# The MLP's second product by Strassen's scheme, its MLP stage issued in a planned order

## The chip, the cores and the metric

The kernel runs on one core of a Trainium2 chip. The metric is device time in microseconds from the start to the end of one execution. TensorE (PE) multiplies, with its weight loads (PEld) alongside; VectorE (DVE), ScalarE (ACT) and GpSimd (POOL) do elementwise work; SyncE (SP) issues most of the transfers.

## The reference: what is computed

One decoder layer on x of 512 tokens x 1024 channels, all in float32. A normalised x is projected; half of the columns go through block-sparse attention, half through a causal convolution; both are joined, projected and added to x. What the change touches is the rest:

```python
hn = rms_norm(h, g_mlp_norm[l])
ff = jnp.square(jax.nn.relu(hn @ w_mlp_in[l]))     # 512x1024 @ 1024x4096
h = h + ff @ w_mlp_out[l]                          # 512x4096 @ 4096x1024
return rms_norm(h, g_final)
```

## The kernel before, in words

Every float32 product is made of three passes. An operand `v` is split into a high part (a cast to fp32r, on ACT) and a low part (`v` minus the high part, on DVE), and `mm3` adds high x high, high x low and low x high in PSUM (lines 263 to 265). So each weight tile costs one cast (L236) and one subtraction (L237) of 128x1024 elements, and each product three matmuls.

The MLP goes through the 4096 hidden channels in 4 chunks of 1024 (`NCH`, `CHUNK` = 8 blocks of 128). In a chunk, 8 hidden blocks are made, each a `block` of 8 x 3 matmuls of 512 columns into one PSUM bank (tiles `ff`), and `relu_square` (L999 to L1003) makes of each the relu on ACT, the square on DVE, the high part on ACT and the low part on DVE. The second product of the chunk follows (`zmm`, tiles `z`): for each half of the 1024 output columns, 4 token tiles x 8 blocks x 3 matmuls of 512 columns, which makes 192 a chunk. DVE adds the four banks of a half to the residual `xr` (L1078). Weights arrive through 4 raw buffers and 3 pairs of split buffers, always in the order of `srcs`.

The order of the MLP's instructions is the order in which the code is written. The stages before it are issued by a planner (`Plan`), which picks the next step from costs, due times and biases by kind (`BIAS`); the MLP is not planned in the kernel before. The last half of the last chunk does one token tile after another, with the last tile in two pieces of 256 columns, so that the final norm (L1087, L1022, L1023, L945, L1032) and the stores of a tile run beside the matmuls of the next.

Of the kernel before, what the change touches and what calls it, by code (L numbers as in the profile page):

```python
# [10 lines left out]
F32 = mybir.dt.float32  # L11
# [6 lines left out]
P = 128  # L18
# [14 lines left out]
SCRATCH = 4096  # L33
CT = 4
# [28 lines left out]
class Plan:  # L63
# [32 lines left out]
    def run(self):  # L96
# [8 lines left out]
        while ready:  # L105
            best, first = [], {}
            for s in ready:
                t = 0.0
                ok = True
                for b in s["uses"]:  # L110
                    if b["tag"] is None:
                        f = self.free[b["kind"]]
                        if len(f) <= (s["keep"] if self.hot else 0):
                            ok = False
                            break
                        t = max(t, min(f.values()))
# [46 lines left out]
def hybrid_layer(ctx: ExitStack, tc: tile.TileContext, x, pack, w_in, w_out, g_mlp, w1, w2, g_fin, out):  # L163
# [34 lines left out]
    for c in range(DFF // P // CHUNK):  # L198
        srcs += [colblock(w1, c * CHUNK + b) for b in range(CHUNK)]
        for hf in range(2):  # L200
            srcs += [rowpair(w2, c * CHUNK + k, hf * 512) for k in range(0, CHUNK, 2)]
# [724 lines left out]

    pm.tile([P, 1456], F32, name="shift")
# [211 lines left out]
```

## Time and profile before

| | us |
|---|---|
| runs | 578.13, 579.93, 1454.63 (median 579.93) |
| the profiled execution's own time | 578.81 |
| its span, first to last instruction | 577.1 |
| PE busy | 562.6 (97%) |
| DVE, ACT, POOL busy | 327.2, 264.9, 143.7 |
| a chunk of the MLP, 307 to 394 us: PE, DVE, ACT, POOL busy | 87.00, 36.12, 25.81, 0.00 |
| from the end of the last matmul to the end of the span | 7.1 |

The profiled execution took 578.81 us, 1.1 less than the median; the run of 1454.63 us stands alone. The granted TensorE clock was 0.996 on average. A busy PE is read with care, since matmuls overlap: the step from one start to the next is what one costs. The rows themselves are below, in numbered groups.

### The profile page before, as it was taken

The page shows a single profiled execution, that of the slowest core. Times are in us where ns is not written, and L with a number is a line of the kernel's source. Part 1 is how long each engine was busy: PE and PEld are TensorE (multiplying, and loading weights), DVE is VectorE, ACT ScalarE, POOL GpSimd, SP SyncE. Part 2 cuts the span into 40 slices and gives each one's busy share as a digit, 9 for nine tenths or more (in the row PEclk, how much of TensorE's full clock was granted, in tenths as well). Part 3 has the DMA queues.
Part 4 walks back from the last instruction along what each step waited for, and adds up shares of the span by engine and source line. Part 5 has one row for each costly group of instructions (what it writes and reads, how often), then busy time and mean ns, then how long its engine had stood idle before and what let it go on. Part 6 is the DMA issues. An engine that isn't in the chain of part 4 may idle for free.

```text
span 577.1 us, 7305 instructions
## 1 busy us (share of the span) xinstructions
PE 562.6 (97%) x2784; PEld 472.4 (82%) x2784; DVE 327.2 (57%) x489; ACT 264.9 (46%) x445; POOL 143.7 (25%) x166
## 2 busy tenths in 40 slices
PE   8999999899899999999999999999999999999995
PEld 7988888787688889988888888888888888888884
DVE  4479889899996764544424444324454324454343
ACT  5776596979875442533212343212343212343223
POOL 2289979599645310000000000000000000000002
PEclk9999999999999999999999999999999999999998
DMA  8443323221131720323332323333223323233103
GB/s 274 137 136 94 101 73 110 68 80 37 37 147 39 218 75 1 123 98 109 108 104 79 104 79 110 110 90 92 91 92 109 110 79 104 82 101 110 37 0 148
DMA packets 58836, 56.20 MB, mean 97 GB/s; under 512 B 1840, under 2 KB 42928, under 8 KB 58800
## 3 DMA queue, kind: packets, MB, share of 16 engines
q1 hardware_dynamic: 58512, 54.68, 30.6%
q10 hardware_dynamic: 288, 1.05, 0.5%
q8 instruction: 22, 0.36, 0.2%
q14 instruction: 14, 0.11, 0.1%
HBM read 53.62 MB, written 2.10 MB: 97 GB/s over the span
## 4 chain that ended last, share of the span: by engine, by line
PE 92%; DVE 2%; ACT 2%; DMA 1%; issue 1%; POOL 0%; SPq 0%; POOLq 0%; ACTq 0%
PE ff L264 10%; PE ff L265 10%; PE ff L263 10%; PE z L264 10%; PE z L263 10%; PE z L265 10%; PE u L263 3%; PE u L264 3%; PE u L265 3%; PE y L263 3%; PE y L265 3%; PE y L264 3%; PE q L265 1%; PE q L263 1%; PE v L263 1%; PE q L264 1%
## 5 line engine op out<-in xcount | busy, mean ns | idle before, releaser
L237 DVE TENSOR_TENSOR wl<-raw,wh 128x1024 fp32r<-128x1024 f32 (+1 forms) x69 | 81.4, 1183 | 94.2 <-ACT wh L236 94.0
L236 ACT CAST wh<-raw 128x1024 fp32r<-128x1024 f32 (+1 forms) x73 | 70.9, 981 | 115.2 <-PE z L265 84.0
L263 PE MATMUL ff<-hTh,wh 128*128 128x512 f32 (+1 forms) x280 | 103.9, 371 | 0.0
L264 PE MATMUL ff<-hTl,wh 128*128 128x512 f32 (+1 forms) x280 | 103.8, 371 | 0.0
L265 PE MATMUL ff<-hTh,wl 128*128 128x512 f32 (+1 forms) x280 | 103.8, 371 | 0.0
L264 PE MATMUL z<-wl,ffh 128*128 128x512 f32 (+1 forms) x264 | 101.0, 383 | 0.0
L263 PE MATMUL z<-wh,ffh 128*128 128x512 f32 (+1 forms) x264 | 101.0, 383 | 0.0
L265 PE MATMUL z<-wh,ffl 128*128 128x512 f32 (+1 forms) x264 | 101.0, 383 | 0.0
L550 POOL TENSOR_TENSOR acc<-acc,ct 128x512 f32<-128x512 f32 x60 | 89.2, 1487 | 11.8 <-ACT ct L547 8.5
L937 POOL TENSOR_SCALAR ms0f<-ms_f 128x1 f32<-128x1 f32 x4 | 0.8, 190 | 328.7 <-ACT f L329 328.7
L263 PEld LDWEIGHTS ff<-hTh,wh 128*128 128x128 f32 x280 | 52.8, 188 | 9.1
L264 PEld LDWEIGHTS ff<-hTl,wh 128*128 128x128 f32 x280 | 52.8, 188 | 9.0
L265 PEld LDWEIGHTS ff<-hTh,wl 128*128 128x128 f32 x280 | 52.8, 188 | 9.0
L1001 DVE TENSOR_TENSOR sq<-rl 128x512 f32<-128x512 f32 x32 | 22.2, 693 | 64.2 <-ACT rl L999 64.2
L263 PEld LDWEIGHTS z<-wh,ffh 128*128 128x128 f32 x264 | 49.6, 188 | 9.8
L264 PEld LDWEIGHTS z<-wl,ffh 128*128 128x128 f32 x264 | 49.6, 188 | 9.7
L265 PEld LDWEIGHTS z<-wh,ffl 128*128 128x128 f32 x264 | 49.6, 188 | 9.6
L999 ACT ACTIVATE rl<-ff 128x512 f32<-128x512 f32 x32 | 19.2, 599 | 82.6 <-PE ff L265 82.6
L566 DVE SCALAR_TENSOR_TENSOR cs<-hin,pk,cs 128x512 f32<-128x512 f32 x58 | 43.5, 750 | 0.9
L547 ACT ACTIVATE ct<-hin,pk 128x512 f32<-128x512 f32 x60 | 40.5, 718 | 2.5 <-POOL acc L550 1.8
L1003 DVE TENSOR_TENSOR ffl<-sq,ffh 128x512 fp32r<-128x512 f32 x32 | 22.2, 694 | 21.9 <-ACT ffh L1002 21.9
L453 ACT CAST wh<-raw 128x1024 fp32r<-128x1024 f32 x21 | 22.0, 1050 | 21.7 <-PE u L264 9.9
(172 smaller groups left out, 926.8 us busy)
## 6 DMA issues: line engine op xcount, KB each, us to landing
raw<-w SPq DMA_DIRECT2D x64, 512.0 KB, 3.7
raw<-w_in SPq DMA_DIRECT2D x18, 512.0 KB, 3.6
raw<-w_out SPq DMA_DIRECT2D x8, 512.0 KB, 3.6
xr<-x SPq DMA_DIRECT2D x4, 512.0 KB, 5.1
out<-ot SPq DMA_DIRECT2D x8, 256.0 KB, 2.0
x<-x SPq DMA_DIRECT2D x4, 256.0 KB, 4.6
raw<-w_in SPq DMA_DIRECT2D x4, 256.0 KB, 6.4
x<-x SPq DMA_DIRECT2D x2, 512.0 KB, 6.6
```

Source lines behind the costliest of these rows:

```text
L236: nc.scalar.copy(hi[:, c], raws[n][:, c])
L237: low.tensor_tensor(lo[:, c], raws[n][:, c], f32(hi[:, c]), op=OP.subtract)
L263: nc.tensor.matmul(ps, sh, mh, start=first, stop=False)
L264: nc.tensor.matmul(ps, sh, ml, start=False, stop=False)
L265: nc.tensor.matmul(ps, sl, mh, start=False, stop=last)
L453: nc.scalar.copy(hi, raws[n])
L547: p = plan.step(f"prod{i}", "act", 0.72, lambda src=src, j=j, ct=ct: nc.scalar.activation(get(ct), src, AF.Copy, scale=wtap(i, j)), needs= ...
L550: s = plan.step(f"tapp{i}", "pool", 1.38, lambda ct=ct: nc.gpsimd.tensor_tensor(get(acc), get(acc), get(ct), op=OP.add), needs=[p, s], use ...
L566: s = plan.step(f"tapd{i}", "dve", 0.78, lambda src=src, j=j, last=last: nc.vector.scalar_tensor_tensor(get(acc) if last else get(cs), src ...
L999: nc.scalar.activation(rl, ps, AF.Relu)
L1001: nc.vector.tensor_mul(sq, rl, rl)
L1003: nc.vector.tensor_sub(ff["l"][:, b], sq, f32(ff["h"][:, b]))
```

## The change

The second product of a chunk is a product of a 512x1024 matrix F by a 1024x1024 matrix W. F is cut into 2x2 blocks of (256 tokens x 512 channels), W into 2x2 blocks of (512 channels x 512 columns), and Strassen's seven products take the place of eight: each is a sum or difference of blocks of F times a sum or difference of blocks of W, 2 token tiles x 4 channel blocks x 3 matmuls of 512 columns. A chunk has 168 of these for 192 before. In turn

- blocks of W are added and subtracted before they are split (`mt1`, `mt3`, `mt4`, `mt6`, `mt7`, two 128x1024 halves each), and 14 tiles of the second product's weights are split, for 8 before (`mb`);
- F is kept as float32, and its 7 operands (5 of them sums or differences, `ms`) are split as 128x1024 tiles (`ma`), where before each of 8 hidden blocks was split at 128x512;
- each product lands in two banks and is added to, or subtracted from, one to two blocks of the residual: 24 additions of 128x512 a chunk for 8 (`mev`);
- the square is one DVE instruction that reads PSUM and the relu.

Every step of the MLP is handed to the planner, with `ON` naming kinds that go to one engine only. As the planner assigns them, 7 sums of a chunk are on POOL (mt3 and mt6 and mt1, two each, and ms7); in the last chunk two low parts as well. The rest is on DVE.

```diff
+ON = {
+    "mal": ("dve",), "ms1": ("dve",), "ms5": ("dve",), "ms6": ("dve",), "ms7": ("pool",), "mt1": ("pool",),
+    "mt3": ("pool",), "mt6": ("pool",), "mt7": ("dve",),
+}
...
+    "low15": -172, "max": -20, "max4": -63, "max5": -116, "max6": -30, "mbh": -377, "mbl": -249.6, "mev": -240.1,
+    "mfo": -646, "ms1": 261, "norm": 453, "os": 122, "os4": -49, "pl": 80, "pl3": -53, "prod": -356,
...
-    pm.tile([P, 1456], F32, name="shift")
+    pm.tile([P, SHIFT], F32, name="shift")
...
-    def relu_square(c, b, ps):
-        rl = pm.tile([P, S], F32, tag="rl", name=f"rl{c}_{b}", bufs=2)
-        nc.scalar.activation(rl, ps, AF.Relu)
-        sq = pm.tile([P, S], F32, tag="sq", name=f"sq{c}_{b}", bufs=2)
-        nc.vector.tensor_mul(sq, rl, rl)
-        nc.scalar.copy(ff["h"][:, b], sq)
-        nc.vector.tensor_sub(ff["l"][:, b], sq, f32(ff["h"][:, b]))
...
+    def combine(kind, out, a, b, op, needs, uses):
+        def fn():
+            e = nc.gpsimd if s["eng_used"] == "pool" else nc.vector
+            e.tensor_tensor(out(), a(), b(), op=op)
+
+        s = plan.step(kind, either(kind), 0, fn, needs=needs, uses=uses, shared=True)
+        return s
+
+    def weights(kind, b, ready, a):
+
+        wb = plan.buffer("w", w_tiles)
+        h = plan.step(f"{kind}h", "act", 1.04, lambda: nc.scalar.copy(get(wb)[0], get(b)), needs=[ready, last.get("high")], uses=[b, wb])
+        last["high"] = h
+        l = low_parts(f"{kind}l", lambda: get(wb)[1], lambda: get(b), lambda: get(wb)[0], [h], [b, wb])
...
+    def operand(kind, ob, i, x, needs, uses):
+
+        hi, lo = (lambda: quarter(ob, i)), (lambda: quarter(ob, i + 1))
+        h = plan.step(f"{kind}h", "act", 1.04, lambda: nc.scalar.copy(hi(), x()), needs=needs, uses=uses + [ob])
+        l = low_parts(f"{kind}l", lo, x, hi, [h], uses + [ob])
...
+    def add_to(t, cols, b, needs, op=OP.add):
+        n = cols.stop - cols.start
+        return plan.step("mev", "dve", dve_cost(n), lambda: nc.vector.tensor_tensor(
+            xt[t][:, cols], xt[t][:, cols], get(b)[:, 0:n], op=op), needs=needs, uses=[b])
...
+        return plan.step("msq", "dve", 0.75, lambda: nc.vector.scalar_tensor_tensor(
+            get(F)[:, b % 4], get(ps), 0.0, get(rl), op0=OP.max, op1=OP.mult), needs=[s], uses=[ps, rl, F])
...
+        s3 = sums("mt3", t3, r12, r22, OP.subtract, [row("12"), row("22")])
+        B[3] = split(t3, s3)
+        s6 = sums("mt6", r12, r12, r11, OP.add, [s3, row("11")])
+        B[6] = split(r12, s6)
+        t4 = [new_tt(f"t4{j}_{c}") for j in js]
+        s4 = sums("mt4", t4, r21, r11, OP.subtract, [row("21"), row("11")])
+        B[4] = split(t4, s4)
+        B[2] = split(r11, row("11"))
+        s1 = sums("mt1", r11, r11, r22, OP.add, [low_of(2), row("22"), s6, s4])
+        B[1] = split(r11, s1)
+        B[5] = split(r22, row("22"))
+        s7 = sums("mt7", r21, r21, r22, OP.add, [s4, row("22")])
+        B[7] = split(r21, s7)
...
-        for hf in range(2):
-            cols = slice(hf * 512, (hf + 1) * 512)
...
-            for kp in range(0, tail, 2):
-                w = unit()
-                for k in (kp, kp + 1):
-                    for ps, (t, pc) in zip(banks, pieces):
-                        zmm(ps, k, t, w, k == 0, k == CHUNK - 1, pc)
...
+        O = {3: operand("ma", ops[0], 0, A(0, 0), k1, [F[0]])}
...
+        mixed(6, 1, 0, 2, A(1, 0), A(0, 0), OP.subtract, k1, [F[0]])
+        O[4] = operand("ma", ops[1], 0, A(1, 1), k2, [F[1]])
+        mixed(2, 0, 1, 2, A(1, 0), A(1, 1), OP.add, k2, F)
+        mixed(1, 1, 2, 0, A(0, 0), A(1, 1), OP.add, k2, F)
+        mixed(5, 0, 2, 2, A(0, 0), A(0, 1), OP.add, k2, F)
+        mixed(7, 1, 3, 0, A(0, 1), A(1, 1), OP.subtract, k2, [F[1]])
...
+                            mm3(get(banks[t])[:, 0:cols.stop - cols.start], ah[:, k, ts], al[:, k, ts], bh[:, kk, cols],
+                                bl[:, kk, cols], k == 0, k == 3)
...
+        spread(3, (0, 1, add), (1, 1, add))
+        spread(6, (1, 1, add))
+        spread(4, (0, 0, add), (1, 0, add))
+        spread(2, (1, 0, add), (1, 1, sub))
+        spread(1, (1, 1, add), (0, 0, add))
+        if not final:
+            spread(5, (0, 0, sub), (0, 1, add))
+            spread(7, (0, 0, add))
+            return
...
+    for c in range(NCH):
+        chunk(c)
+    for s in plan.run():
+        s["fn"]()
```

The products run in the order 3, 6, 4, 2, 1, 5, 7. Each has two halves (j = 0, 1), which need one split weight tile each; a half is 12 matmuls. The instructions of all engines ahead of the MLP stand as before, and so do the matmuls of the first chunk's hidden blocks.

Place 1 is DVE in the third chunk, from the square of the last hidden block up to the last operand that the first products need. Before, behind the last square and its low part, only the low parts of weights and the four residual additions follow:

```order
L1001 TENSOR_TENSOR sq_7_4016<-rl_7_4014 128x512
L1003 TENSOR_TENSOR ffl_3723<-sq_7_4016,ffh_3722 128x512
L237 TENSOR_TENSOR wl_4025<-raw_3877,wh_4024 128x1024
L237 TENSOR_TENSOR wl_4055<-raw_3914,wh_4054 128x1024
L237 TENSOR_TENSOR wl_4085<-raw_3951,wh_4084 128x1024
L237 TENSOR_TENSOR wl_4115<-raw_3988,wh_4114 128x1024
L1078 TENSOR_TENSOR xr<-xr,z_4020 128x512
```

Now twelve instructions of 128x1024 follow the last square, which itself writes F_2_4033. The first two are the sums for products 1 and 2; op... are low parts of operands of F (opxl of products 4 and 2, opffh of 1 and 5); wl<-r_2_3886 is the second half's weight of product 6, t_2_... those of product 4, r_3884 and r_3925 those of product 2:

```order
L1066 TENSOR_TENSOR temp_4002<-F_2_3882,F_2_4033 128x1024
L1066 TENSOR_TENSOR temp_4143<-F_2_3882,F_2_4033 128x1024
L1058 TENSOR_TENSOR opxl<-F_2_4033,opxl 128x1024
L1058 TENSOR_TENSOR opffh<-temp_4002,opffh 128x1024
L1058 TENSOR_TENSOR opxl<-temp_4143,opxl 128x1024
L1058 TENSOR_TENSOR wl<-r_2_3886,wh 128x1024
L1066 TENSOR_TENSOR temp_4143<-F_2_3882,F_2_4033 128x1024
L1058 TENSOR_TENSOR wl<-t_2_3998,wh 128x1024
L1058 TENSOR_TENSOR wl<-t_2_4068,wh 128x1024
L1058 TENSOR_TENSOR opffh<-temp_4143,opffh 128x1024
L1058 TENSOR_TENSOR wl<-r_3884,wh 128x1024
L1058 TENSOR_TENSOR wl<-r_3925,wh 128x1024
```

What moved: the low part that product 6 needs halfway stands sixth behind the last square, and those of product 2 eleventh and twelfth.

Place 2 is the weight of product 1. It is a sum that POOL writes over r_3884 and r_3925 once product 2's low parts have been made of them, and behind it POOL has the sum for product 7. POOL's whole list for the third chunk (before, POOL had nothing in the MLP until the final norm):

```order
L1066 TENSOR_TENSOR t_2_3888<-r_2_3845,r_2_3879 128x1024
L1066 TENSOR_TENSOR r_2_3845<-r_2_3845,r_3884 128x1024
L1066 TENSOR_TENSOR t_2_3955<-r_2_3886,r_2_3921 128x1024
L1066 TENSOR_TENSOR r_2_3886<-r_2_3886,r_3925 128x1024
L1066 TENSOR_TENSOR r_3884<-r_3884,r_2_3879 128x1024
L1066 TENSOR_TENSOR r_3925<-r_3925,r_2_3921 128x1024
L1066 TENSOR_TENSOR temp_4002<-F_2_4033 128x1024
```

On DVE, the two low parts of product 1's weight stand among residual additions (m_4153 is product 6, m_4191 product 4); four additions of product 3 (m_4108, m_4112) stand ahead of these rows:

```order
L1092 TENSOR_TENSOR xr<-xr,m_4153 128x512
L1092 TENSOR_TENSOR xr<-xr,m_4157 128x512
L1092 TENSOR_TENSOR xr<-xr,m_4191 128x512
L1058 TENSOR_TENSOR wl<-r_3884,wh 128x1024
L1092 TENSOR_TENSOR xr<-xr,m_4195 128x512
L1092 TENSOR_TENSOR xr<-xr,m_4191 128x512
L1058 TENSOR_TENSOR wl<-r_3925,wh 128x1024
L1058 TENSOR_TENSOR wl<-r_2_3879,wh 128x1024
```

What moved: a weight that was a load, a cast and a subtraction now waits for DVE, then POOL, then ACT, then DVE again.

Place 3 is the end on DVE. Before, the last token tile alone is left when the last matmuls run:

```order
L1087 TENSOR_TENSOR xr<-xr,z_4729 128x256
L945 SCALAR_TENSOR_TENSOR ot_4716<-xr,fr_4865,gfinbc 128x512
L1087 TENSOR_TENSOR xr<-xr,z_4730 128x256
L1022 SCALAR_TENSOR_TENSOR fs_768_4903,ms_f_768_4904<-xr 128x256
L1023 TENSOR_TENSOR fn_768_4902<-ms_f_768_4904,fn_512_4884 128x1
L945 SCALAR_TENSOR_TENSOR ot_4724<-xr,fr_4907,gfinbc 128x512
```

Now (m_4950 and m_4982 are the first tile and the first half of the second tile of product 7, mlast the second half; ahead of these rows stand the four additions of product 5, one of product 1 and one scaled output):

```order
L1092 TENSOR_TENSOR xr<-xr,m_4950 128x512
L1145 TENSOR_TENSOR ot_4989<-xr,gfinbc 128x512
L1092 TENSOR_TENSOR xr<-xr,m_4982 128x256
L1145 TENSOR_TENSOR ot_4989<-xr,gfinbc 128x512
L1179 SCALAR_TENSOR_TENSOR ot_4989<-xr,fr_2538,gfinbc 128x512
L1092 TENSOR_TENSOR xr<-xr,mlast 128x256
L1145 TENSOR_TENSOR ot_5036<-xr,gfinbc 128x512
L1166 SCALAR_TENSOR_TENSOR fs_256_5040,ms_f_256_5039<-xr 128x256
L1168 TENSOR_TENSOR fn_256_2542<-ms_f_256_5039,fn_0_2541 128x1
L1145 TENSOR_TENSOR ot_5036<-xr,gfinbc 128x512
L1179 SCALAR_TENSOR_TENSOR ot_5036<-xr,fr_2540,gfinbc 128x512
L1179 SCALAR_TENSOR_TENSOR ot_5036<-xr,fr_2543,gfinbc 128x512
```

What moved: more of the final norm stands behind the last matmul on DVE, and the stores of two tiles instead of one.

## Rows read from the trace of the kernel before

**Rows 1.** The page's busy us, share of the span and instructions of each engine.

```profile
PE 562.6 (97%) x2784; PEld 472.4 (82%) x2784; DVE 327.2 (57%) x489; ACT 264.9 (46%) x445; POOL 143.7 (25%) x166
```

**Rows 2.** The page's chain of waits that ended last, share of the span by engine.

```profile
PE 92%; DVE 2%; ACT 2%; DMA 1%; issue 1%; POOL 0%; SPq 0%; POOLq 0%; ACTq 0%
```

**Rows 3.** Stretches: length, busy us (instructions) of PE, PEld, DVE, ACT, POOL; clock, DMA share, GB/s.

```profile
307.00:394.00 87.00, 87.00 (x386) 72.06 (x384) 36.12 (x41) 25.81 (x32) 0.00 (x0) 1.00 0.32 97
...
139.00:148.00 9.00, 7.58 (x51) 5.85 (x49) 8.65 (x23) 7.92 (x20) 8.20 (x11) 1.00 0.35 118
```

**Rows 4.** Instructions on PE in order of time: start us, us, what; second and third chunk's first matmul.

```profile
308.32 0.39 PE L263 MATMUL ff<-hTh,wh 128*128 128x512 f32 x1
...
395.36 0.39 PE L263 MATMUL ff<-hTh,wh 128*128 128x512 f32 x1
```

**Rows 5.** Groups by line and shape: count, busy us, mean ns, idle before.

```profile
L237 DVE TENSOR_TENSOR wl<-raw,wh 128x1024 fp32r<-128x1024 f32 x65 | 79.6, 1225 | 94.1 <-ACT wh L236 94.0
L1001 DVE TENSOR_TENSOR sq<-rl 128x512 f32<-128x512 f32 x32 | 22.2, 693 | 64.2 <-ACT rl L999 64.2
L1078 DVE TENSOR_TENSOR xr<-xr,z 128x512 f32<-128x512 f32 x28 | 19.1, 687 | 7.6 <-PE z L265 7.6
L728 DVE SCALAR_TENSOR_TENSOR vhl<-v,r,vhl 128x512 fp32r<-128x512 f32 x4 | 3.0, 748 | 0.8 <-ACT vhl L725 0.8
L236 ACT CAST wh<-raw 128x1024 fp32r<-128x1024 f32 x65 | 68.3, 1050 | 115.2 <-PE z L265 84.0 <-DVE xr L1078 17.5 <-issue 10.2
L457 POOL TENSOR_TENSOR wl<-raw,wh 128x1024 fp32r<-128x1024 f32 x1 | 2.4, 2406 | 0.0
```

**Rows 6.** In order of time, behind one hidden block: PE's next matmul, ACT, DVE.

```profile
400.80 0.39 PE L263 MATMUL ff<-hTh,wh 128*128 128x512 f32 x1
...
401.00 0.60 ACT L999 ACTIVATE rl<-ff 128x512 f32<-128x512 f32 x1 [4.38 <-PE ff L265]
...
401.63 0.69 DVE L1001 TENSOR_TENSOR sq<-rl 128x512 f32<-128x512 f32 x1 [3.76 <-ACT rl L999]
```

**Rows 7.** In order of time, DVE instructions one behind the other.

```profile
41.52 1.55 DVE L566 SCALAR_TENSOR_TENSOR cs<-hin,pk,cs 128x512 f32<-128x512 f32 x2
...
85.65 1.22 DVE L457 TENSOR_TENSOR wl<-raw,wh 128x1024 fp32r<-128x1024 f32 x1
86.78 0.75 DVE L566 SCALAR_TENSOR_TENSOR cs<-hin,pk,cs 128x512 f32<-128x512 f32 x1
87.44 0.69 DVE L685 TENSOR_TENSOR ql<-tpq,qs 128x512 fp32r<-128x512 f32 x1
```

**Rows 8.** Single lines in the convolution stage: duration ns min/median/max, first and last start.

```profile
L457 DVE TENSOR_TENSOR wl<-raw,wh x20: 1214/1352/2328, 26.7 to 142.1; 128x1024 fp32r<-128x1024 f32 x20
...
L550 POOL TENSOR_TENSOR acc<-acc,ct x60: 1272/1295/2244, 32.0 to 142.5; 128x512 f32<-128x512 f32 x60
```

**Rows 9.** In order of time, DVE reading PSUM beside POOL's one 128x1024 instruction.

```profile
177.26 2.94 DVE L865 TENSOR_SCALAR y<-cp,mv,r_ln 128x512 f32<-128x512 f32 x4
...
178.55 2.41 POOL L457 TENSOR_TENSOR wl<-raw,wh 128x1024 fp32r<-128x1024 f32 x1
```

**Rows 10.** In order of time, the end: last matmuls, DVE's last instructions, the last store's issue.

```profile
569.59 0.28 PE L264 MATMUL z<-wl,ffh 128*128 128x256 f32 x1
569.71 0.28 PE L265 MATMUL z<-wh,ffl 128*128 128x256 f32 x1
...
570.36 0.42 DVE L1087 TENSOR_TENSOR xr<-xr,z 128x256 f32<-128x256 f32 x1
...
572.31 0.75 DVE L945 SCALAR_TENSOR_TENSOR ot<-xr,fr,gfinbc 128x512 f32<-128x512 f32 x1 [0.67 <-POOL fr L1027]
...
573.49 0.37 SPq L1034 DMA_DIRECT2D out<-ot  x1
```

**Rows 11.** The page's transfers: KB each, median us from issue to landing.

```profile
raw<-w SPq DMA_DIRECT2D x64, 512.0 KB, 3.7
out<-ot SPq DMA_DIRECT2D x8, 256.0 KB, 2.0
```

More of the change, by code (lines that the diff above doesn't have):

```diff
@@ L109, in run @@
                 ok = True
[L110 to L116, printed above, removed]
+                new = [b["kind"] for b in s["uses"] if b["tag"] is None]
+                for kind in new:
+                    f = sorted(self.free[kind].values())
+                    n = new.count(kind)
+                    if len(f) < n + (s["keep"] if self.hot else 0):
+                        ok = False
+                        break
+                    t = max(t, f[n - 1])
                 if not ok:
@@ L1029, in final_store, with either @@
[L1029 to L1038 removed]
+    def either(kind):
+        costs = {"dve": 1.23, "pool": 2.45}
+        return {e: costs[e] for e in ON.get(kind, costs)}
@@ new lines, in hybrid_layer, with load, low_parts @@
+    last = {}
+    def load(kind, b, src):
+        last["load"] = plan.step(kind, "sp", 1.95, lambda: nc.sync.dma_start(
+            get(b).rearrange("p (a b) -> p a b", a=src.shape[1]), src), needs=[last.get("load")], uses=[b])
+        return last["load"]
+    def low_parts(kind, lo, x, hi, needs, uses):
+        def fn():
+            e = nc.gpsimd if l["eng_used"] == "pool" else nc.vector
+            e.tensor_tensor(lo(), x(), f32(hi()), op=OP.subtract)
+        l = plan.step(kind, either(kind), 0, fn, needs=needs, uses=uses, shared=True)
+        return l
@@ new lines, in final_store @@
+    def final_store(t, d, ready, ot):
+        e = D2 if d is D1 else D1
+        r = stat(f"fr{t}")
+        s = plan.step("mfr", "pool", 0.55, lambda: nc.gpsimd.tensor_tensor(r, msq[t], mhalf, op=OP.pow), needs=[ready])
+        b = ot_b[t // 2]
+        s2 = plan.step("mfz", "dve", 0.75, lambda: nc.vector.scalar_tensor_tensor(
+            ot()[:, e], xt[t][:, e], r, gfi_b["t"][:, e], op0=OP.mult, op1=OP.mult), needs=[s], uses=[b], shared=True)
+        s1 = plan.step("mfy", "act", 0.7, lambda: nc.scalar.activation(ot()[:, d], ot()[:, d], AF.Copy, scale=r),
+                       needs=[s, last["mfo", t]], uses=[b])
+        for s, cols in ((s1, d), (s2, e)):
+            plan.step("mst", "sp", 0.5, lambda cols=cols: nc.sync.dma_start(out[t * P:(t + 1) * P, cols], ot()[:, cols]),
+                      needs=[s], uses=[b])
@@ L1055, in hybrid_layer @@
+            plan.step("mgf", "act", 0.4, load_gains, needs=[sq[0]])
         for b in range(b0, CHUNK):
[L1056 to L1093 removed]
@@ new lines, in pair, with spread @@
+        def pair(m):
+            return [ps_buffer(f"m{m}{c}{t}") for t in range(2)]
+        done = {}
+        def spread(m, *parts):
+            banks = pair(m)
+            s = product(m, banks)
+            for i, d, op in parts:
+                for t in range(2):
+                    done.setdefault((2 * i + t, d), []).append(add_to(2 * i + t, (D1, D2)[d], banks[t], [s], op=op))
+        add, sub = OP.add, OP.subtract
+        spread(3, (0, 1, add), (1, 1, add))
+        spread(6, (1, 1, add))
@@ new lines, in chunk @@
+        spread(5, (0, 1, add), (0, 0, sub))
+        half = {t: final_half(t, D2, done[t, 1], otile[t]) for t in range(2)}
+        banks = pair(7)
+        s = product(7, banks, tiles=(0,))
+        s = add_to(0, D1, banks[0], [s] + done[0, 0])
+        final_store(0, D2, final_ssq(0, D1, [s], half[0], True), otile[0])
+        for n in range(2):
+            cols = slice(n * 256, (n + 1) * 256)
+            ps = banks[1] if n == 0 else ps_buffer("mlast")
+            s = product(7, {1: ps}, tiles=(1,), cols=cols)
+            s = add_to(1, cols, ps, [s] + done[1, 0])
+            half[1] = final_ssq(1, cols, [s], half[1], n == 1)
```

268 lines of the change are left out of this document (185 added, 83 removed), and 7 rows, old and new, of the table BIAS.

## The prediction, blind

> **What bounds the kernel now.** I read the page's busy shares first: PE is busy 97% of the span, DVE 57%, ACT 46%, POOL 25% [rows 1]. Busy PE time overlaps itself, so the chain of waits came next: 92% of it is PE [rows 2]. Then the stretches: in a chunk of the MLP PE works without a gap at a granted clock of 1.00, the higher of its two levels (2.4 GHz), while DVE has 36.1 of 87 us of work, ACT 25.8 and POOL none [rows 3]. The price of a matmul is the step between starts: from the first one of the second chunk to that of the third lie 384 matmuls in 87.04 us, 0.2267 us each [rows 4]. So the time of the MLP is its count of matmuls times 0.2267 us, and everything else has room.
>
> **What goes.** 192 matmuls of the second product become 168 in each of four chunks: 4 x 24 x 0.2267 = **21.8 us** less on the path. The rate should stay, since a matmul still has 512 columns, fp32r operands and a weight load of its own. The Trainium skill ("TensorE: Matmul & The Clock Gate", section "Wait — 56ns, not 53.3ns?") gives 215.7 ns from start to start for 512 columns at the full clock, measured on bf16; by it the saving would be 20.7 us, an estimate from that page. The row shows 227 ns for this kernel's fp32r matmuls, and the measurement decides. Off the path go 8 casts and 8 low parts of hidden blocks a chunk on ACT and DVE.
>
> **What comes, in total.** A chunk now has 360 matmuls, 81.6 us. For DVE I count 37 instructions of 128x1024, 8 squares and 24 additions. Behind one another, 128x1024 costs 1.13 us (85.65 to 86.78) and a 512-wide one 0.66 (86.78 to 87.44) [rows 7], so about 0.09 below the durations of 1.225, 0.748 and 0.687 [rows 5]: 37 x 1.14 + 8 x 0.66 + 24 x 0.60 = 61.9 us. The square's form (PSUM and SBUF in) is priced by the nearest row, 748 ns [rows 5]; 693 is the other end [rows 5], 0.4 us a chunk, and changes nothing. POOL gets 7 sums of 2.41 us [rows 5], 16.9 us. ACT has 29 casts of 1.05 and 8 relus of 0.60 [rows 5, 6], 35.3 us. Each is under 81.6, DVE and POOL together (78.8) too, but barely. Whether POOL's share counts against DVE is the question: in the convolution stage a DVE subtraction of two SBUF tensors took 1214 ns at least and up to 2328, POOL's own 128x512 sum 1295 and up to 2244 [rows 8]. Each waits for the other's whole instruction, once (2328 - 1225 = 1103, under one POOL sum). DVE instructions that read PSUM ran beside POOL's 2.41 us undisturbed, at 0.74 each [rows 9]. The squares and additions read PSUM, 19.7 us a chunk, which can lie beside POOL. So the load fits, and what is left are places where something is due before DVE has come to it.
>
> **Place 1, product 6.** Let 0 be the start of product 3. The relu starts 0.20 us after the hidden block's last matmul gave way (401.00 against 400.80), the square 0.63 later (401.63) [rows 6], at 0.83. A dependent DVE instruction starts 0.05 behind its forerunner's end (two in 1.55 where one takes 0.75) [rows 7], so the first of the twelve starts at 0.83 + 0.75 + 0.05 = 1.63. The low part that product 6 needs for its second half is the sixth: it starts at 1.63 + 5 x 1.14 = 7.33 and is ready at 8.6. PE gets there after 36 matmuls, 8.16. PE waits **0.45 us**.
>
> **Place 2, product 1.** The other six follow at 1.14: product 2's low parts end at 14.3 and 15.4. Only then POOL may sum over the first; DVE's twelfth holds it up to 15.4. POOL: 15.4 to 17.8 and 17.8 to 20.2. ACT casts the first to 18.9; its low part, on DVE, waits for POOL's second sum and runs 20.2 to 21.45. PE has four products before it, 4 x 5.44 + 0.45 = 22.2: in time. The second cast ends at 21.3; DVE makes the two additions that stand ahead, to 22.6, but POOL took its seventh sum at 21.45 and holds DVE to 23.85; the low part ends at 25.1. PE needs it at 22.2 + 2.72 = 24.9. PE waits **0.2 us**, rounded up to 0.25 for the hand-over. If the two engines did not exclude each other, this wait would be nil; so its ends are 0 and the 1.7 us of the second rival below.
>
> Together 0.7 us a chunk, **2.8 us** in four.
>
> **Other cover.** The loads are as many and as large as before, 512 KB each. The next chunk's first buffers come free at 21.5 and 25.1, a load lands 3.7 us later [rows 11], cast and low part take 2.3, so its first weight is there at about 28 while it is needed at 38.8. If that 10 us cover went, each us late would be a us of PE. Banks: product 1 reuses those of product 3, whose additions end at 17.8, needed at 22.2.
>
> **The end.** Before, the last matmul starts at 569.71 and gives way 0.12 later (the step of its kind), DVE's last instruction ends at 573.06 (3.2 behind PE), the last store is issued at 573.49 and the span ends 3.6 us after that [rows 10]. Now call product 5's end E. Behind it DVE has five additions (5 x 0.60), a scaled output (0.66) and the five rows of place 3 ahead of mlast (0.60 + 0.60 + 0.34 + 0.60 + 0.66): 6.5 us from E + 0.2, while product 7's matmuls take 5.44. DVE is about 1.1 us late at mlast. From mlast on it has 0.34 + 0.60 + 0.34 + 0.25 (an allowance for the one-element sum) + 0.60 + 0.66 + 0.75 = 3.5, and ends at E + 10.2, 4.8 behind PE: +1.6. Four stores of 256 KB, not two, wait at the end. Beside a landing of 2.0 us for a store stands one of 3.7 for a load of twice the size [rows 11]: 256 KB more cost between nothing (all in flight together) and 1.7, two stores more between 0 and 3.4. I take 0.9, nearer to the lower end, since part of the 3.7 is latency that stores share. **+2.5 us**, ends 0 and 5.
>
> **Sum.** -21.8 + 2.8 + 2.5 = -16.5. From the profiled execution's 578.8 us this gives 562.3. That execution lies 1.1 us under the median of the runs shown, so I put **563 us**.
>
> **The rivals.**
>
> 1. *No new wait on PE.* DVE is a little quicker, or POOL and DVE overlap, and the tail costs little. For it: the waits are a few tenths against prices rounded up. Against: place 1 has no POOL in it, and 0.45 us would have to come out of six instructions. 578.8 - 21.8 + 2.5 = 559.5, without the tail 557.
>
> 2. *POOL keeps the shared access.* POOL's seventh sum is queued right behind its sixth. If POOL takes the access again before the waiting DVE low part, this one runs 22.6 to 23.85, product 1 starts 1.7 us late, and then its second half is in time: 2.15 us a chunk, 8.6 in all: 578.8 - 21.8 + 8.6 + 2.5 = 568.1. The Trainium skill ("SBUF — State Buffer", section "SBUF: two separate sides") calls the access an exclusive lock which whoever starts first holds for the whole instruction, the other fully blocked; it names no order among those who wait, and by it this could happen. Against it: no DVE row waited longer than one POOL sum though POOL's sums stood back to back there [rows 8]. A DVE that is 3% dearer in its long stretch makes place 1 0.7 and place 2 about as bad, so 568 to 572 is where several small misses land.
>
> 3. *DVE becomes the bound: slower.* With DVE and POOL at 78.8 us beside PE's 81.6, 2.8 us more per chunk fills the room. If each of DVE's 69 instructions waited like the dependent pair (0.80 from start to start for 0.66, +0.14) [rows 7], that is +9.7: 88.5 us a chunk, if nothing of POOL's 16.9 lay beside DVE, against 87.0 before. Four chunks then lose 6 us, the end 2.5: 587.3. It decides from 81.6 on, and the gain is gone at about 86.5. Against: most neighbours in the lists do not depend on each other, and 19.7 us of PSUM reads can lie beside POOL [rows 9].
>
> 4. *The change does not do what it says*, a matmul gets dearer than 0.2267. At 0.24 the 1440 matmuls of the MLP would take 19 us more: 581.4. There is no sign of it: weight load and moving operand keep their sizes. Short waits don't lower the clock either: with 7.58 of 9 us busy between 139 and 148 it stayed at 1.00 [rows 3].
>
> **How the numbers follow.** Chances: the forecast 0.50 (559 to 567, from its ends), no new wait 0.13, POOL keeping the access or DVE a little late 0.23, DVE as the bound 0.07, dearer matmuls 0.02, something unforeseen 0.05. About 2%, 11.6 us, is what a measurement here can tell from no change, so faster means under 568.3. That takes the forecast nearly whole (0.48), the first rival (0.13) and a third of the second (0.08): 0.69. Slower by 2% (over 591.5) takes half of the third and some of the unforeseen: 0.05. The rest, 0.26, is within. The range takes the forecast, most of rival 1 and rival 2 up to 571: 558 to 571.
>
> **What would show it.** The count of product matmuls should be 672 at 0.227 from start to start. In PE's waits, two per chunk: at product 6's second half and at product 1, on DVE's low parts, 0.2 to 0.7 us each; if product 1's is 1.5 or more, POOL kept the access. DVE's busy time in a chunk should be 68 to 75 us and POOL's 17 to 25, with sums stretched where they meet DVE. From the last matmul to the span's end, 8.5 to 10.5 us. What would make me wrong: waits of PE at every product, or DVE without idle time through a chunk.

## The result and the profile after

The changed kernel took **559.23 us** (median of four runs, 558.63 to 560.06) against 579.03 for the kernel before on the same chip; the ratio is **0.9666**, 95% interval 0.9637 to 0.9695; it leaves out the one run of before that took 1454.63 us. Forecast were 563 us in a range of 558 to 571. The profiled execution has a span of 557.5 us, 19.6 less than before's 577.1.

The page of the changed kernel, busy us and share of the span of each engine, then the chain of waits that ended last:

```profile
PE 540.6 (97%) x2676; PEld 452.3 (81%) x2676; DVE 444.1 (80%) x603; ACT 296.6 (53%) x465; POOL 228.7 (41%) x196
...
PE 91%; DVE 3%; ACT 2%; issue 1%; DMA 1%; POOL 0%; SPq 0%; ACTq 0%; POOLq 0%
```

Against [rows 1, 2]: PE has 22.0 us less and the same share, DVE 117 us more, POOL 85 more. DVE went from 57% to 80% of the span, and the chain still is PE. By stretches (two of 82 us, about a chunk each; columns as in [rows 3]):

```profile
306.00:388.00 82.00, 82.00 (x362) 67.59 (x361) 65.81 (x70) 33.92 (x37) 19.62 (x7) 1.00 0.34 103
388.00:470.00 82.00, 82.00 (x362) 67.62 (x361) 64.55 (x70) 33.85 (x37) 19.43 (x7) 1.00 0.34 103
```

PE is busy all the time and the granted clock stays at 1.00 (2.4 GHz). DVE has 65 of 82 us, POOL 19.5: together more than the stretch is long, so they overlap.

What busy time can't show is a short wait between overlapping matmuls. It is read from the steps between starts. PE in order of time, the MLP's first matmul, the third chunk around product 6's second half, and the last matmul:

```profile
218.56 0.28 PE L268 MATMUL ff<-hTh,wh 128*128 128x256 f32 x1
...
435.62 0.39 PE L270 MATMUL m<-wh,opxh 128*128 128x512 f32 x1
435.84 0.39 PE L268 MATMUL m<-wh,opxh 128*128 128x512 f32 x1
436.20 0.50 PE L269 MATMUL m<-wl,opxh 128*128 128x512 f32 x1
436.53 0.39 PE L270 MATMUL m<-wh,opxh 128*128 128x512 f32 x1
436.76 0.39 PE L268 MATMUL m<-wh,opxh 128*128 128x512 f32 x1
...
548.08 0.28 PE L270 MATMUL mlast<-wh,opffl 128*128 128x256 f32 x1
```

The steps are 0.22, **0.36, 0.33**, 0.23: the first matmul that reads the weight's low part (`wl`, L269) is late, and the pair loses 0.24 us. The same pair stands in each of the four chunks (272.43, 354.30, 436.20, 518.06), and one of 0.11 at 544.41 on a low part of POOL's; no other step of the MLP is more than 0.02 us longer than its like in the kernel before. The waits name the releaser (engine, tile and line waiting <- who ended it: us in total, times, longest):

```profile
POOL r L1066 <- DVE wl L1058: 136.8, 4, 37.2
...
PEld m L269 <- DVE wl L1058: 1.5, 4, 0.4
...
PEld m L269 <- POOL wl L1058: 0.3, 1, 0.3
```

PEld waits 0.4 us each time, partly under the matmul ahead, so PE loses only 0.24. POOL's 136.8 us of waiting cost nothing: it stands idle until product 2's low parts are done.

Product 1, the second place of the forecast, does not wait. The third chunk, where product 3 starts at 427.68, DVE in order of time, and then POOL:

```profile
428.51 0.69 DVE L1109 SCALAR_TENSOR_TENSOR F<-ff,rl 128x512 f32<-128x512 f32 x1 [3.27 <-ACT rl L1108]
429.24 2.36 DVE L1066 TENSOR_TENSOR temp<-F,F 128x1024 f32<-128x1024 f32 x2
...
434.92 1.22 DVE L1058 TENSOR_TENSOR wl<-r,wh 128x1024 fp32r<-128x1024 f32 x1
...
440.60 2.35 DVE L1058 TENSOR_TENSOR wl<-r,wh 128x1024 fp32r<-128x1024 f32 x2
442.87 4.27 DVE L1092 TENSOR_TENSOR xr<-xr,m 128x512 f32<-128x512 f32 x7
447.06 1.60 DVE L1058 TENSOR_TENSOR wl<-r,wh 128x1024 fp32r<-128x1024 f32 x1
...
449.78 3.37 DVE L1058 TENSOR_TENSOR wl<-r,wh 128x1024 fp32r<-128x1024 f32 x2
```

```profile
441.96 5.61 POOL L1066 TENSOR_TENSOR r<-r,r 128x1024 f32<-128x1024 f32 x2 [35.26 <-DVE wl L1058]
447.54 3.40 POOL L1066 TENSOR_TENSOR temp<-F 128x1024 f32<-128x1024 f32 x1
```

Read by turns. POOL's first sum was held until DVE's twelfth instruction was done (5.61 for two of 2.41). DVE's low part at 447.06 took 1.60 for 1.22: held until POOL's second sum ended at 447.57. POOL's seventh sum then took 3.40 for 2.41: held by that low part. The next low part was held by the seventh sum (3.37 for two). The access changed hands each time, and nobody had it twice while the other waited.

The end, DVE in order of time:

```profile
548.45 0.74 DVE L1179 SCALAR_TENSOR_TENSOR ot<-xr,fr,gfinbc 128x512 f32<-128x512 f32 x1
549.11 0.41 DVE L1092 TENSOR_TENSOR xr<-xr,mlast 128x256 f32<-128x256 f32 x1
549.44 0.68 DVE L1145 TENSOR_TENSOR ot<-xr,gfinbc 128x512 f32<-128x512 f32 x1
...
551.25 1.41 DVE L1179 SCALAR_TENSOR_TENSOR ot<-xr,fr,gfinbc 128x512 f32<-128x512 f32 x2
```

and the issue of the last store, on SP's queue:

```profile
553.58 0.41 SPq L1184 DMA_DIRECT2D out<-ot  x1
```

The last matmul gives way at 548.20 (its start and the 0.12 us step of its kind), but `mlast` is added at 549.11: DVE is late by its queue, not by PE. It ends 4.46 us behind PE (3.23 before, [rows 10]) and the span 9.30 behind (7.27; the 7.1 of the table before counts that matmul's modelled length instead of its step). The last four stores are issued one behind the other, at 552.17, 552.60, 553.08 and 553.58; the last is 0.92 us behind DVE's end, where before it was 0.43 (573.49 for 573.06).

The 19.6 us are therefore: 96 matmuls -21.8, waits +1.1, end +2.0, and an MLP that began 0.9 us earlier (218.56 for 219.44) in this execution.

For every profiled execution of this and the runs below I take three numbers: the MLP's first matmul, the length from there to the end of the last matmul, and the rest of the span. The medians are from more than one chip; the ratios given with each run are to the kernel before on the same chip.

| kernel | first | MLP | end | median of runs |
|---|---|---|---|---|
| before | 219.44 | 350.39 | 7.27 | 579.03 |
| changed | 218.56 | 329.64 | 9.30 | 559.23 |
| changed, again | 217.76 | 329.72 | 9.32 | 558.69 |
| product 4 twice | 218.37 | 351.22 | 8.61 | 580.49 |
| before, 24 fewer a chunk | 219.48 | 328.57 | 7.25 | 557.04 |
| low part last | 218.45 | 328.52 | 9.43 | 558.47 |
| low part last, again | 220.23 | 328.53 | 9.44 | 559.54 |
| all sums on DVE | 217.57 | 345.23 | 8.10 | 573.41 |
| 11 sums on POOL | 221.72 | 329.54 | 8.94 | 560.27 |
| tile 0's output on POOL | 217.63 | 328.53 | 9.14 | 557.12 |
| tile 3's output on POOL | 221.40 | 328.87 | 8.63 | 557.66 |
| both on POOL | 219.85 | 328.88 | 9.07 | 559.51 |

### The profile page after: what moved, and what is told of

It is laid out like the page before. It is cut to its first block, busy times and chain, and to the rows that moved or that the text cites. A ratio compares the mean times of both kernels' runs of the same rounds, so it can differ in the third digit from the quotient of the medians.

```text
span 557.5 us, 7335 instructions
## 1 busy us (share of the span) xinstructions
PE 540.6 (97%) x2676; PEld 452.3 (81%) x2676; DVE 444.1 (80%) x603; ACT 296.6 (53%) x465; POOL 228.7 (41%) x196
## 4 chain that ended last, share of the span: by engine, by line
PE 91%; DVE 3%; ACT 2%; issue 1%; DMA 1%; POOL 0%; SPq 0%; ACTq 0%; POOLq 0%
PE ff L270 10%; PE ff L269 10%; PE ff L268 10%; PE m L269 9%; PE m L270 9%; PE m L268 9%; PE u L268 3%; PE u L269 3%; PE u L270 3%; PE y L268 3%; PE y L270 3%; PE y L269 3%; PE q L270 1%; PE q L268 1%; PE v L268 1%; PE q L269 1%
## 5 line engine op out<-in xcount | busy, mean ns | idle before, releaser
L269 PE MATMUL ff<-hTl,wh 128*128 128x512 f32 (+1 forms) x280 | 103.9, 371 | 0.0
L1066 POOL TENSOR_TENSOR r<-r,r 128x1024 f32<-128x1024 f32 x16 | 45.3, 2841 | 142.7 <-DVE wl L1058 136.8
L1074 ACT CAST wh<-raw 128x1024 fp32r<-128x1024 f32 x29 | 30.6, 1055 | 79.0 <-PE ff L269 59.0
L1074 ACT CAST wh<-r 128x1024 fp32r<-128x1024 f32 x40 | 41.7, 1051 | 44.7 <-POOL r L1066 25.7
L1058 DVE TENSOR_TENSOR wl<-raw,wh 128x1024 fp32r<-128x1024 f32 x29 | 42.7, 1472 | 26.4 <-ACT wh L1074 26.3
L1092 DVE TENSOR_TENSOR xr<-xr,m 128x512 f32<-128x512 f32 x96 | 59.5, 676 | 0.9 <-PE m L270 0.9
L269 PEld LDWEIGHTS ff<-hTl,wh 128*128 128x128 f32 x280 | 52.8, 188 | 9.1
L1066 POOL TENSOR_TENSOR t<-r,r 128x1024 f32<-128x1024 f32 x8 | 20.0, 2505 | 90.1 <-DMA r<-w 89.9
L1058 DVE TENSOR_TENSOR wl<-r,wh 128x1024 fp32r<-128x1024 f32 x38 | 50.3, 1353 | 0.8 <-ACT wh L1074 0.8
L1109 DVE SCALAR_TENSOR_TENSOR F<-ff,rl 128x512 f32<-128x512 f32 x32 | 21.9, 685 | 33.5 <-ACT rl L1108 33.5
L458 ACT CAST wh<-raw 128x1024 fp32r<-128x1024 f32 x21 | 22.1, 1050 | 21.7 <-PE u L269 9.9
L462 DVE TENSOR_TENSOR wl<-raw,wh 128x1024 fp32r<-128x1024 f32 x20 | 30.1, 1507 | 1.8 <-ACT wh L458 1.7
L268 PE MATMUL u<-xh,wh 128*128 128x256 f32 (+1 forms) x88 | 29.7, 338 | 0.0
L269 PE MATMUL u<-xl,wh 128*128 128x256 f32 (+1 forms) x88 | 29.4, 334 | 0.0
```

The costliest lines, as they stand in the source:

```text
L268: nc.tensor.matmul(ps, sh, mh, start=first, stop=False)
L269: nc.tensor.matmul(ps, sh, ml, start=False, stop=False)
L458: nc.scalar.copy(hi, raws[n])
L462: e.tensor_tensor(lo, raws[n], f32(hi), op=OP.subtract)
L1058: e.tensor_tensor(lo(), x(), f32(hi()), op=OP.subtract)
L1066: e.tensor_tensor(out(), a(), b(), op=op)
```

## The experiments

My theory was the forecast's: the time is the count of matmuls times their step, plus the few places where an operand is late, plus the end. The rivals were that DVE and POOL set the pace of the MLP, and that the shared access is the cost.

**Product 4 twice, and 24 matmuls fewer without Strassen.** The first puts the 96 matmuls back into the changed kernel; the second takes as many out of the kernel before and leaves a channel block out of its result.

```diff
+            if m == 4:
+                product(m, banks)
             s = product(m, banks)
```

```diff
                 for k in (kp, kp + 1):
+                    if k == 3:
+                        continue
```

> The changed kernel, but product 4 of each of the four chunks issues its 24 matmuls twice (the second set starts its banks anew, so the first set's result is not used). That is 96 matmuls more, as many as the change took away. My theory, that the time is the count of matmuls times their step of 0.2267 us plus short waits and the end: 559.2 + 21.8 = 581.0 us (580 to 582), ratio to the kernel before 1.002 to 1.006, the step at 0.2267 and the end at 9.3 us as in the changed kernel. Rival, that the MLP runs at the pace of VectorE and GpSimd and TensorE merely keeps step with them: the 96 matmuls would be absorbed in part, below 575 us.

> The kernel before, with channel block 3 of 8 left out of the MLP's second product in every chunk (24 matmuls a chunk, both halves of the columns). It has the changed kernel's count of matmuls and none of its sums, splits and additions. My theory, that a removed matmul is worth its step and that all the added work costs the changed kernel only its short waits and a longer end (1.1 + 2.0 us by the two traces, less a start of the MLP that was 0.9 earlier): 579.0 - 21.8 = 557.2 us (556.5 to 558), 1 to 3 us below the changed kernel. Rival, that the added work costs nothing: 559.2, the same as the changed kernel. Rival, that it also slows the matmuls: 554 or less here.

Measured: 580.49 us, ratio to before 1.0044 (1.0023 to 1.0065); and 557.04 us, ratio 0.9645 (0.9625 to 0.9665). The MLP is 21.6 us longer than the changed kernel's (351.22 for 329.64) and 21.8 shorter than before's (328.57 for 350.39). A matmul is worth its step in both directions, so DVE and POOL do not set the pace. The second kernel's MLP is 1.07 us shorter than the changed one's and its end 2.05: that is the whole price of the sums, splits and additions that Strassen's scheme adds. In the first kernel DVE has 5.44 us more time in the last chunk, too, and ends 3.77 behind PE, not 4.46: 0.7 of DVE's 1.2 us of added delay come from the work that it still has in its queue.

**The weight's low part read last.** Does product 6 wait for the low part because it reads it second of three?

```diff
-  mm3(..., ah[:, k, ts], al[:, k, ts], bh[:, kk, cols], bl[:, kk, cols], k == 0, k == 3)
+  o = get(banks[t])[:, 0:cols.stop - cols.start]
+  nc.tensor.matmul(o, ah[:, k, ts], bh[:, kk, cols], start=k == 0, stop=False)
+  nc.tensor.matmul(o, al[:, k, ts], bh[:, kk, cols], start=False, stop=False)
+  nc.tensor.matmul(o, ah[:, k, ts], bl[:, kk, cols], start=False, stop=k == 3)
```

> The changed kernel with the passes of the seven products in another order: high x high, operand's low part x weight's high, and the weight's low part last (in the changed kernel it is the first or second matmul of a half that reads it). My theory: TensorE waits at product 6's second half because the weight's low part comes 0.24 us late, measured at the second matmul of the half; read one matmul later it has 0.227 us more, so the wait falls from 0.24 to 0.02 us a chunk or nothing, and 0.11 us at product 7 of the last chunk goes too: 559.2 - 1.0 = 558.2 us (557.7 to 558.7). Rival, that TensorE's weight loads ahead of the matmuls already need the low part, so that the order of the passes does not matter: 559.2, with 0.24 us a chunk still in the trace.

The same place of the third chunk in this kernel, PE in order of time (L1306 is the one that reads `wl`):

```profile
434.78 0.39 PE L1305 MATMUL m<-wh,opxh 128*128 128x512 f32 x1
435.01 0.39 PE L1306 MATMUL m<-wl,opxh 128*128 128x512 f32 x1
435.23 0.39 PE L1304 MATMUL m<-wh,opxh 128*128 128x512 f32 x1
435.46 0.39 PE L1305 MATMUL m<-wh,opxh 128*128 128x512 f32 x1
435.69 0.40 PE L1306 MATMUL m<-wl,opxh 128*128 128x512 f32 x1
435.93 0.39 PE L1304 MATMUL m<-wh,opxh 128*128 128x512 f32 x1
```

Every step is 0.22 to 0.24: the wait is gone, in all four chunks, and the MLP takes 328.52 us, as long as the one without any of the added work. So the matmul waited only for what it reads itself, and a grace of one step was enough. PEld still waits for `wl` four times, 0.2 us at most, but under the matmul ahead. The median was 558.47, but the gain could not be told from the spread. So both kernels ran once more, on one chip:

> The changed kernel once more, unchanged, on one chip with the next run, since the gain of the run with the weight's low part last (558.47 against 559.23 us) is smaller than what two chips can tell. By the traces 559.2 us (558.5 to 560), with 0.24 us of wait a chunk at product 6's second half. The stages ahead of the MLP, the same in all these kernels, ended between 217.6 and 219.5 us in the profiled executions; if that is the spread of single executions, the two profiles of this kernel differ in it too; if it belongs to the built program, the first matmul of the MLP starts at 218.6 again.

> The run with the weight's low part last once more, beside the changed kernel on the same chip. My theory: 1.0 us below it (0.5 to 1.3), no wait at product 6. Rival, that a wait taken away inside a chunk comes back at the end, where VectorE is the late one: no difference.

Measured: 558.69 us for the changed kernel (ratio 0.9662, 0.9640 to 0.9683) and 559.54 with the low part last (0.9677, 0.9653 to 0.9701). The traces repeat to 0.1 us: 329.72 and 328.53 for the MLP. What differs is the first column: the same program reached the MLP at 218.56 and 217.76, the other at 218.45 and 220.23. My expectation of a faster time failed; that the wait goes, and saves 1.1 us inside the MLP, is shown. Of the rival little is left: the end is 0.12 us longer (9.44 for 9.32).

Over all twelve executions the MLP begins between 217.57 and 221.72, though the stages ahead of it are the same work in the same order. The traces show two parts of that. The first lies in the first 25 us, while the first loads arrive: an instruction of DVE in the changed kernel starts 0.20 us earlier than its like in the kernel before at 6.0 us, 0.54 at 9.7 and 0.87 at 18.4, and that stays so up to the MLP. DVE's first instruction on tile `u` starts between 23.97 and 26.61 us in the twelve, and from there to the MLP ten of them take 193.6 us. The other two take 195.1: those with 11 sums on POOL and with tile 3's output on POOL. In these alone the granted clock between 150 and 160 us was 0.83 and 0.84, and 1.00 in the ten others. PE had been busy 0.72 and 0.66 of the 2 us up to 150; in the run with both on POOL it was 0.66 too, and the clock stayed at 1.00. What makes the loads differ, and what lowered the clock in these two, stays open.

**All sums on DVE.** In the table of kinds, POOL is taken away.

```diff
-  "ms7": ("pool",), "mt1": ("pool",), "mt3": ("pool",), "mt6": ("pool",),
+  "ms7": ("dve",), "mt1": ("dve",), "mt3": ("dve",), "mt6": ("dve",),
```

> The changed kernel with all sums of blocks on VectorE (in the changed kernel 7 of a chunk are on GpSimd). VectorE then has 65.8 + 7 x 1.2 = 74 us of work in a chunk of 82, so by the total it fits. My theory: it is late all the same, because the work is due in one stretch: from product 3's start it has the twelve (13.7), two sums and two low parts for product 1 (4.6) and ten additions (6.0), some 26 us from 1.6 on, before product 1's second half at 25, and after that the sum and low part for product 7. TensorE waits 1 to 4 us a chunk, at products 1, 5 or 7: 563 to 575 us. Rival, that the access GpSimd and VectorE share is what delays VectorE (it was held by 0.4 to 2.2 us at a time), so that VectorE alone is as quick or quicker: 558 to 559.5, no wait of TensorE longer than 0.3.

573.41 us, ratio 0.9922 (0.9894 to 0.9950), 14.7 more than the changed kernel's 558.69 on the same chip: most of the gain is gone. PE and DVE in the second chunk, in order of time:

```profile
356.59 0.39 PE L268 MATMUL m<-wh,opxh 128*128 128x512 f32 x1
359.21 0.50 PE L269 MATMUL m<-wl,opxh 128*128 128x512 f32 x1 [2.23 <-DVE wl L1058]
...
362.62 0.50 PE L269 MATMUL m<-wl,opxl 128*128 128x512 f32 x1 [0.39 <-DVE wl L1058]
```

```profile
349.26 0.69 DVE L1109 SCALAR_TENSOR_TENSOR F<-ff,rl 128x512 f32<-128x512 f32 x1 [3.27 <-ACT rl L1108]
...
355.67 1.22 DVE L1066 TENSOR_TENSOR temp<-F 128x1024 f32<-128x1024 f32 x1
356.81 1.22 DVE L1066 TENSOR_TENSOR temp<-F,F 128x1024 f32<-128x1024 f32 x1
357.94 1.21 DVE L1058 TENSOR_TENSOR wl<-r,wh 128x1024 fp32r<-128x1024 f32 x1
359.08 1.22 DVE L1058 TENSOR_TENSOR opffl<-temp,opffl 128x1024 fp32r<-128x1024 f32 x1
```

The planner, with ms7 on DVE, put that sum and one more ahead of product 6's low part: it is the eighth instruction behind the square, not the sixth. Two more of 1.13 us and the 0.12 that it was late already make 2.38; the step from 356.59 to 359.21 has 2.39 over 0.227. With 0.11 behind it, 0.66 at product 4 and 0.65 at product 1, which waits for an addition to empty its bank, it is 3.8 us in each of the first three chunks, and 5.0 in the last, where product 1 waits 1.9. The size was forecast, the place mostly not: I had put it at products 1, 5 and 7, and 3.2 of the 3.8 are at 6 and 4. The rival, that DVE is quicker without POOL, falls: DVE was never held here, has 67 of 82 us in such a stretch, and PE waits all the same. The total of the load did not decide; what stood ahead of one instruction did. The run changes both the load and the planner's order, so it is the rows, not the time, that tell the two apart.

**Eleven sums on POOL.**

```diff
-  "mt7": ("dve",),
+  "mt7": ("pool",), "mt4": ("pool",),
```

> The changed kernel with four more of a chunk's sums on GpSimd (those for products 4 and 7), 11 in place of 7: GpSimd then has some 27 to 30 us of work a chunk and VectorE 61. These sums depend on loads alone, so they can run while VectorE waits for squares. My theory: VectorE is not the one that is late in most places, so nothing is gained: the wait at product 6 stays at 0.24 us a chunk, and where GpSimd's sums meet VectorE's subtractions before product 1, TensorE can wait 0 to 2 us in a chunk; 559 to 563 us. Rival, that VectorE's load is what still costs time: less work for it shortens the waits and the end, 557.5 to 558.5 us.

560.27 us, ratio 0.9661 (0.9628 to 0.9695). DVE has 62 us of work in a stretch of 82, POOL 30; the MLP takes 329.54, as in the changed kernel; the wait at product 6 is 0.28 in three chunks and none in the first. Less work on DVE gained nothing inside the MLP, as expected; the end is 0.36 us shorter in this one trace, which the times can't tell. The wait of up to 2 us did not come.

**The end.** VectorE's tail is a queue without gaps, so I moved output multiplications (128x512) to POOL: tile 0's, tile 3's, both, always with the low part last.

```diff
-  last["mfo", t] = plan.step("mfo", "dve", 0.69, lambda: nc.vector.tensor_mul(ot()[:, d], ...
+  mo = {"pool": 1.3} if t == 0 else {"dve": 0.69}        # t == 3; t in (0, 3)
+  mo_s = last["mfo", t] = plan.step("mfo", mo, 0, mfo, needs=ready, ...
```

> As the run with the weight's low part last, and in the last chunk one of the four output multiplications (128x512, token tile 0) on GpSimd in place of VectorE. My theory: behind TensorE's last matmul VectorE works without idle time up to its last instruction, so its end comes sooner by the one instruction, 0.60 us, unless GpSimd's multiplication (1.3 us) holds up one of VectorE's or one of GpSimd's own one-column steps: 557.6 us (557.2 to 558.2), VectorE's last instruction 3.9 us behind TensorE's last matmul for 4.46. Rival, that the stores set the end and not VectorE: no change against the run with the low part last, 558.2.

> The weight's low part last, and in the last chunk the output multiplication of token tile 3 (not of tile 0) on GpSimd, ahead of its two low parts for product 7, at about 534 to 538 us, where it stands idle. In the run with tile 0's, GpSimd's 1.30 us held one of VectorE's scaled outputs (1.41 us for 0.74), which took the 0.60 us back. My theory: here it can hold one of VectorE's subtractions, which are not yet late for anyone, so VectorE ends 0.6 sooner behind the last matmul (4.0 us for 4.6); the low part for product 7 comes up to 1.3 us later and may cost TensorE up to 0.7: between 557.5 and 558.6 us, against 558.2 without the move. Rival, that the access held costs VectorE the same here: 558.2 or more, VectorE's end 4.6 us behind the last matmul.

> The weight's low part last, and in the last chunk two output multiplications on GpSimd: token tile 3's (as in the run before, where VectorE ended 4.44 us behind the last matmul and the span 8.63) and token tile 0's. My theory: VectorE has one instruction of 0.60 us less in its saturated tail, but GpSimd's second multiplication stands among its small steps and holds a scaled output by 0.67, as it did with tile 0's alone: from the last matmul to the span's end 8.5 to 8.8 us, no better than with tile 3's alone, 557.3 us (556.5 to 558.5). Rival, that each multiplication taken away shortens the end: 8.0 us, about 557.0.

Tile 0's: 557.12 us, 0.9645 (0.9629 to 0.9661), but DVE ended 4.68 behind PE, no sooner. DVE, then POOL:

```profile
543.77 1.41 DVE L1184 SCALAR_TENSOR_TENSOR ot<-xr,fr,gfinbc 128x512 f32<-128x512 f32 x1
545.10 0.67 DVE L1092 TENSOR_TENSOR xr<-xr,m 128x512 f32<-128x512 f32 x1
```

```profile
543.33 1.30 POOL L1149 TENSOR_TENSOR ot<-xr,gfinbc 128x512 f32<-128x512 f32 x1 [0.15 <-DVE xr L1092]
```

The scaled output took 1.41 for 0.74: held by POOL's multiplication for 0.67, more than the 0.60 that the move took away. My theory had the caveat and got the outcome wrong; the time lies just under my 557.2 to 558.2, for another reason. Against the first run with the low part last the profiled execution's span is 1.1 us shorter: 0.8 of an earlier MLP and 0.3 of a shorter end.

Tile 3's: 557.66 us, 0.9644 (0.9618 to 0.9669). A row of POOL, and DVE's last one:

```profile
539.02 2.15 POOL L1149 TENSOR_TENSOR ot<-xr,gfinbc 128x512 f32<-128x512 f32 x1 [2.97 <-DVE xr L1092]
```

```profile
553.96 0.75 DVE L1184 SCALAR_TENSOR_TENSOR ot<-xr,fr,gfinbc 128x512 f32<-128x512 f32 x1 [0.67 <-POOL fr L1182]
```

Here POOL was the one held (2.15 for 1.30), while DVE did its subtraction. DVE ended 4.44 behind PE, the span 8.63, and product 7 waited 0.29. I had expected 4.0 for DVE: it did get rid of the instruction, but its last one now waits 0.67 us for POOL's `fr`, as in the kernel before ([rows 10]), so only 0.2 of the 0.6 came through. The rest of the shorter end lies behind DVE's last instruction, where two stores and not four are left to be issued. MLP and end together are 337.5 us, against 338.9 in the changed kernel and 335.8 in the kernel without the added work: the best of the full kernels by the trace. By its time (0.9644 against 0.9662 on the same chip, intervals that overlap) it can't be told from the changed kernel.

Both: 559.51 us, 0.9659 (0.9638 to 0.9681). DVE, then POOL:

```profile
550.01 1.74 DVE L1184 SCALAR_TENSOR_TENSOR ot<-xr,fr,gfinbc 128x512 f32<-128x512 f32 x1
```

```profile
549.94 1.26 POOL L1149 TENSOR_TENSOR ot<-xr,gfinbc 128x512 f32<-128x512 f32 x1
```

Held again, 1.00 us where I had expected 0.67, by POOL's second multiplication from 549.94 to 551.20. The end was 9.07, not the 8.5 to 8.8 that I had expected: worse than with tile 3's alone (8.63). The time lies outside my 556.5 to 558.5, too.

## Why the prediction was right, step by step

- **The step and the count.** Right. From product 6's late matmul of the second chunk (354.30) to that of the third (436.20) lie 360 matmuls in 81.90 us, 0.2275 with 0.24 us of wait, 0.2268 without. The 672 product matmuls are there, and the two counting experiments show 21.6 and 21.8 us for 96.
- **Place 1, 0.45 us forecast, 0.24 measured.** The mechanism was right; three sizes were off, and in part they cancel. The square with PSUM and relu as inputs took 0.69, not the 0.75 that I took from the nearest row, and the sixth instruction ends 8.46 behind product 3's start, not 8.6. And I let PE wait at the first matmul of the half, which reads the high parts alone; the low part is read by the second, 0.227 later. With the measured 8.46 and the right matmul the wait would be 8.46 - 8.16 - 0.227 = 0.07. The rest is what the forecast had no term for: 0.06 from the low part's end (436.14) to the matmul's start (436.20), and 0.10 by which the step behind it is longer than 0.227. So the wait that was measured is made of other parts than the one forecast.
- **Place 2, 0.2 to 0.25 forecast, none measured.** The chain of hand-overs ran as I wrote it: behind product 3's start, POOL's two sums end at 19.9 (forecast 20.2), the first low part at 21.0 (21.45), the second at 24.3 (25.1). PE reads that one at 25.0 (452.66). The forecast lay within a few tenths at each link, and the wait that was left was a difference of two such numbers. Here, too, I let PE wait at the first matmul of the half; by the forecast's own numbers the second reads the low part at 22.2 + 2.72 + 0.23 = 25.15, when it is there (25.1).
- **The end, +2.5 forecast, +2.0 measured**: DVE +1.2 (forecast 1.6) and +0.8 (0.9) from there to the last landing. The order was as forecast; DVE's steps of 0.60 from start to start left it 0.9 us late at `mlast` (1.1). The 0.8 is near the forecast's 0.9 for another reason than the forecast's: 0.5 of it is the issue of four stores one behind the other, and 0.3 the longer way from the last issue to the span's end (3.9 us for 3.6). The forecast had put all of it on the transfers.
- **DVE's load**, 68 to 75 us forecast, was 65: below the range, since POOL held it less than allowed for. POOL's 19.5 lies within.
- **Rival 1** (no new wait, 559.5) came nearest by its number, and held for product 1 but not for product 6; 0.9 us of its nearness lies ahead of the MLP, belongs to no step and is luck. **Rival 2** falls by the hand-overs above: POOL did not keep the access. **Rivals 3 and 4** fall with the counting runs. Rival 4's sentence that short waits don't lower the clock holds for its row and for the MLP, not everywhere: see the two runs with 0.83 and 0.84 above.
- Against the forecast sum of 562.3 the profiled execution took 559.28: 1.7 less of waits, 0.5 less at the end, 0.9 less ahead of the MLP. The median, 559.23, lies at the lower edge of the forecast's own 559 to 567.

## What to carry to other kernels

Where one engine is busy 97% and its steps are even, cost a change by counting that engine's instructions; then look for the operands that come late, and count the instructions queued ahead of each, not the load of the engine that makes it. A wait sits on the instruction that reads the late operand, so reading it one step later gives cover: here it took away 0.24 us a chunk. A total that comes out right can hide terms that cancel, so compare the terms, each with its own row. When a stage gains 1 us and the whole varies by 4 ahead of that stage, compare the stage, and don't claim the time.

## What the runs showed of the hardware that was not expected

- Where two instructions of DVE and POOL exclude each other, the access alternated: in one chunk POOL's sums took 3.40 for 2.41 and DVE's low parts 1.60 and 3.37 (for two), each held once. The Trainium skill ("SBUF — State Buffer", section "SBUF: two separate sides") has the exclusive lock for the whole instruction, and these rows agree; the turn-taking is what these rows add.
- The multiply-by-scalar-and-tensor form on DVE was held, too, where both its tensors lie in SBUF: beside POOL's multiplication in the tail one took 1.41 and one 1.74 us for 0.74. In the convolution stage, where one of its two tensors (`cs`) lies in a PSUM bank, it was not: three took 2.34 us, 0.78 each, in the midst of POOL's sums, and none of the changed kernel's 58 of that line took more than 0.757. The two rows, DVE and then POOL:

```profile
91.72 2.34 DVE L571 SCALAR_TENSOR_TENSOR cs<-hin,pk,cs 128x512 f32<-128x512 f32 x3
```

```profile
85.38 9.48 POOL L555 TENSOR_TENSOR acc<-acc,ct 128x512 f32<-128x512 f32 x6 [1.65 <-ACT ct L552]
```

- The square as one instruction that reads PSUM and SBUF took 0.684 us (median), as much as the form before that read SBUF alone (0.693, [rows 5]).
